# Weight sums of two feed-forward tiles moved from engines to adding DMAs, block sums of the normed tokens moved to VectorE, two results written in place

## The chip, the cores and the metric

The kernel runs on one core of one Trainium2 chip. The metric is the device time of one execution in microseconds, given as the median over runs; less is better. Arithmetic is fp32; for the matmuls every operand is split into a high and a low part of type fp32r.

## The reference, cut to what matters

An encoder trunk of two layers works on 512 + 256 tokens of width 1024. Each layer has a mixer (attention and an mLSTM, side by side), a residual with layer norm, a gated feed-forward of width 2816 with a convolution over three neighbouring tokens, and a second residual with layer norm. The change is all in the feed-forward and in the step into it:

```python
x = _layer_norm(ALPHA * x + mix, ln1_g, ln1_b)
gu = x @ w_gu
gate, up = gu[..., :D_FF], gu[..., D_FF:]
conv = conv_b + sum(gp[:, j:j + S] * conv_w[j] for j in range(CONV_WIDTH))   # gp: gate, padded by a token at each end
hmid = gelu(conv) * up
x = _layer_norm(ALPHA * x + hmid @ w_down, ln2_g, ln2_b)
```

## The kernel before, in words

The 768 tokens are 6 token tiles of 128, the feed-forward's width is 22 tiles of 128. Each operand of a matmul stands twice, as a high part and as the remainder, and each product takes three passes (high by high, high by low, low by high).

The gate and up products of one feed-forward tile are one two-by-two block product in Strassen's form: with the token halves (tiles 0 to 2 and 3 to 5) and the two halves of the contraction there are seven products `p1` to `p7` of 12 matmuls each (`product`, line 967) instead of eight. Their operands are sums. On the weights' side four are needed for each feed-forward tile: t1 = u0 + g0, t2 = u1 + t1, t3 = u1 + u0, t4 = g1 + t2. On the tokens' side there are four sums for each token tile of the second half (`combine`, lines 905 to 908), made once in a layer. `ff_tile` puts the seven results together: the copy `m1` of `p1` (line 979, ScalarE), `u2`, `u4`, `u3` (lines 988, 989, 992) and from these the halves of `g` and `up` (lines 983, 993, 996, 999), all on VectorE, then the convolution (lines 1000 to 1003), gelu (1004), the product (1005) and its split (1009, 1010). After every three tiles `down` (line 1027) adds their part of the second product to the accumulator.

Class `Weights` brings the weights. Pieces of 128 x 512 are loaded in a fixed order on SyncE's queue into a ring of six raw slots (line 143). Each block is then converted: ScalarE makes the high part (line 186), VectorE the remainder (line 187), into one of 12 slots. Sums are made in two ways. For feed-forward tiles 1 and 2 (`ENG`) engines make them from raw pieces (`_value`, line 164): t1 and t3 on GpSimd, t2 and t4 on VectorE, into one buffer `E` or over a raw piece. For all other tiles a DMA on SyncE's queue copies one summand into a slot `T` (line 152), and a DMA on GpSimd's queue adds the other (line 153). There are four slots `T` (`NSUM`); the load of a sum waits until the sum four places earlier has been converted. They exist from the start of the output projection of the mixer to the end of the feed-forward.

Step into the feed-forward: the second half of the output projection (`wo`, line 923) goes over the token tiles in the order 0, 1, 3, 2, 4, 5. For each, VectorE adds the residual (926), takes statistics (865, 870), GpSimd makes the inverse deviation (871, 872), and VectorE applies the norm (876, 882). Then `combine` makes the four sums of tiles 3, 4 and 5, on VectorE for the tiles in `VT` and else on GpSimd. Two token tiles later the blocks are transposed on TensorE (386), and split on ScalarE (388) and VectorE (389). The first two products of feed-forward tiles 0 and 1 (`FF_EARLY`) are started ahead of the rest.

The order on each engine is set when the program is built: an instruction's priority is its place in the code, shifted by `prio` (conversions are put back by 100, the first products forward by 50). An engine then works in that order. PSUM banks are taken in turn by tag (`FTAGS`: three `d`, two `s`, one `L`), so a product waits until the results of an earlier one have been read. In `ff_tile` every buffer exists once; the copy `m1` of tile 1 waits for the last reader of `m1` of tile 0.

Of the kernel before, what the change touches and what calls it, by code (L numbers as in the profile page):

```python
# [13 lines left out]
F32 = mybir.dt.float32  # L14
F32R = mybir.dt.float32r
AF = mybir.ActivationFunctionType
ALU = mybir.AluOpType
# [16 lines left out]
HALF = T // 2  # L34
# [49 lines left out]
WO_K = (4,5,0,1,6,7,2,3)  # L84
WO_ORDER0 = (0, 1, 2, 3, 4, 5)
NSG = 3
NSUM = 4
ENG = (1, 2)
AT1 = 11
AT2 = 8  # L90
AT3 = 12
FF_EARLY = 2
WO_ORDER = (0,1,3,2,4,5)
LAG1 = 2
VT = (5,)


class Weights:

# [15 lines left out]

    def block(self, src, n, dst=None):
        self.blocks.append((src, n, dst))  # L120
        for x in (src["a"], src["b"]) if isinstance(src, dict) and src["engine"] else (src,):
            if not isinstance(x, dict):
                self.uses[x] += 1

    def sum(self, layer, a, b, engine=None, over=None):

        s = {"a": a, "b": b, "engine": engine, "layer": layer, "read": False, "over": over}
        if engine is None:
            self.sums.append(s)
        return s  # L130

    def unit(self, ap, n=1024):
# [5 lines left out]
    def _load(self):  # L138

        while self.n_dma < len(self.dram) and (self.n_dma < NRAW or self.uses[self.n_dma - NRAW] == 0):  # L140
# [4 lines left out]
            self.n_dma += 1  # L145
        while self.diff_pool is not None and self.n_sum < len(self.sums) and (self.n_sum < NSUM or self.sums[self.n_sum - NSUM]["read"]):
            s = self.sums[self.n_sum]
            if s["layer"] != self.layer:
                break
            s["tile"] = t = self.diff_pool.tile([128, 512], F32, tag="T", name=f"T{self.n_sum}", bufs=NSUM)  # L150
            self.n_sum += 1
# [1 line left out]
            self.nc.gpsimd.dma_start(t, s["b"]["tile"] if isinstance(s["b"], dict) else s["b"], accum_op=ALU.add)  # L153

    def _value(self, src, n):
        if isinstance(src, dict):
            if "tile" not in src:

                v = [x["tile"] if isinstance(x, dict) else self.raw[x] for x in (src["a"], src["b"])]
                if isinstance(src["b"], dict) or src["over"]:  # L160
                    src["tile"] = v[1]
                else:
                    src["tile"] = self.diff_pool.tile([128, 512], F32, tag="E", name=f"E{self.n_conv}", bufs=1)
                src["engine"].tensor_tensor(out=src["tile"], in0=v[0], in1=v[1], op=ALU.add)
                for x in (src["a"], src["b"]):
                    if not isinstance(x, dict) and x != src["over"]:
                        self.uses[x] -= 1
            return src["tile"]
        return self.raw[src]

    def _conv(self, i):
        src, n, dst = self.blocks[i]
        self._load()
        v = self._value(src, n)
        if callable(dst):
            dst(v)
            self.uses[src] -= 1
            return
        if dst is None:
            h = self.hl_pool.tile([128, WCOL], F32R, tag="wh", name=f"wh{i}")[:, :n]  # L180
            l = self.hl_pool.tile([128, WCOL], F32R, tag="wl", name=f"wl{i}")[:, :n]
            self.hl[i] = (h, l)
        else:
            h, l = dst
            v = v.rearrange("p (k t) -> p k t", k=4)
        self.nc.scalar.activation(h, v, AF.Identity)  # L186
        self.nc.vector.tensor_tensor(out=l, in0=v, in1=h.bitcast(F32), op=ALU.subtract)  # L187
        if isinstance(src, dict):
            src["read"] = True
            if src["over"]:  # L190
                self.uses[src["over"]] -= 1
        else:
            self.uses[src] -= 1
        self._load()

    def pump(self):

        live = sum(1 for j in range(self.n_done, self.n_conv) if self.blocks[j][2] is None)
        while self.n_conv < len(self.blocks):
            if isinstance(self.blocks[self.n_conv][0], dict):  # L200
                self._load()
                if self.diff_pool is None or ("tile" not in self.blocks[self.n_conv][0] and not self.blocks[self.n_conv][0]["engine"]):
                    break
            if self.blocks[self.n_conv][2] is None:
                if live >= NSLOT:
                    break
                live += 1
            with self.prio(self.urgency):
                self._conv(self.n_conv)
            self.n_conv += 1  # L210
# [16 lines left out]
def trunk(ctx, nc, tc, d, o, depth=DEPTH):  # L227
    V, S, G, PE = nc.vector, nc.scalar, nc.gpsimd, nc.tensor
# [18 lines left out]
    def P(tag, name):  # L247
        return pp.tile([128, 512], F32, tag=tag, name=name, bufs=banks[tag])
# [10 lines left out]
    W = Weights(nc, wr, wh, prio)  # L259
# [27 lines left out]
    for l in range(depth):  # L287
        if l:
            for u in range(4):
                W.unit(d["w_c1"][l, u], 1056)  # L290
        for u in range(4):
            W.unit(d["w_av"][l, u])
        for h in range(4):
            W.unit(d["w_aq"][l, h])
            W.unit(d["w_ak"][l, h])
            if h == 0 or h == (1 if L1 else 2):
                for u in range(4):
                    W.unit(d["w_lv" if h == 0 else "w_lo"][l, u])
        for hf in range(2):
            for u in range(4):  # L300
                W.unit(d["w_out"][l, hf, u])
        early = {}
        for i in range(FF_EARLY):
            early[i] = [W.piece(d["w_g"][l, i, :, p * 512:(p + 1) * 512], 512) for p in range(2)]
            for src in early[i]:
                W.block(src, 512)
        for kind, i in ffn_seq:
            if kind == "f":


                def at(w, p):
                    return d[w][l, i, :, p * 512:(p + 1) * 512]

                g0, g1 = early[i] if i in early else [W.piece(at("w_g", p), 512) for p in range(2)]
                if i in ENG:
                    u0, u1 = [W.piece(at("w_u", p), 512) for p in range(2)]
                    t1 = W.sum(l, u0, g0, G)
                    t2 = W.sum(l, u1, t1, V)
                    t3 = W.sum(l, u1, u0, G, over=u0)
                    t4 = W.sum(l, g1, t2, V)  # L320
                else:
                    u1 = W.piece(at("w_u", 1), 512)
                    t1 = W.sum(l, at("w_u", 0), at("w_g", 0))
                    t2 = W.sum(l, at("w_u", 1), t1)
                    t3 = W.sum(l, at("w_u", 1), at("w_u", 0))
                    t4 = W.sum(l, at("w_g", 1), t2)
                for src in (t1, t2, t3, t4, u1) if i in early else (g0, g1, t1, t2, t3, t4, u1):
                    W.block(src, 512)
            else:
                f0, f1 = FF_GROUPS[i]  # L330
                for hf in range(2):
                    for f in range(f0, f1):
                        W.block(W.piece(d["w_down"][l, f, :, hf * 512:(hf + 1) * 512], 512), 512)
# [58 lines left out]
    for l in range(depth):  # L392
# [503 lines left out]
        def combine(t):  # L896
# [5 lines left out]
            x0, x1 = acc[:, t - 3, 0:512], acc[:, t - 3, 512:1024]  # L902
            E = V if t in VT else G
            s1, s2, s3, s4 = (sp.tile([128, 512], F32, tag=f"S{i}", name=f"S{i}_{t}") for i in (1, 2, 3, 4))
# [11 lines left out]
        for hf in range(2):  # L916
            order = (WO_ORDER0, WO_ORDER)[hf]
            units = [W.take() for _ in range(8)]
            for j, t in enumerate(order):
                p = P("d", f"wo{hf}{t}")  # L920
# [28 lines left out]
        ft = FT.enter_context(tc.tile_pool(name=f"ft{l}", bufs=1, reuse_waits="tile"))  # L949
# [8 lines left out]
        def bank(name):  # L958
            n_bank[0] += 1
            return P(tags[(n_bank[0] - 1) % 6], name)[:, 0:HALF]  # L960

        def product(ps, x):

            blk = W.take()
            for k in range(4):
                for i, (a, b) in enumerate(PASSES):
                    PE.matmul(ps, blk[1 + a][:, k * 128:(k + 1) * 128], x[:, k, b, :], start=k + i == 0, stop=k == 3 and i == 2)  # L967
            W.done(blk)

        def ff_tile(f):  # L970
            w0, w1, w2, cb = (convw[:, l, f, i:i + 1] for i in range(4))
            g = ft.tile([128, T], F32, tag="g", name=f"g{f}")
            up = ft.tile([128, T], F32, tag="up", name=f"up{f}")
            c = ft.tile([128, T], F32, tag="c", name=f"c{f}")
            m1, u2, u3, u4 = (ft.tile([128, HALF], F32, tag=t, name=f"{t}_{f}") for t in ("m1", "u2", "u3", "u4"))
            lo_, hi_ = slice(0, HALF), slice(HALF, T)
            p1 = bank(f"p1_{f}")
            product(p1, A11)
            S.copy(m1, p1)
# [26 lines left out]
            s = f % RING  # L1006
# [5 lines left out]
        def down(gi):  # L1012
# [5 lines left out]
            for hf, t in ([(hf, t) for t in range(NT) for hf in range(2)] if last else [(hf, t) for hf in range(2) for t in range(NT)]):  # L1018
# [18 lines left out]
                if last and hf:  # L1037
# [8 lines left out]
                    else:  # L1046
                        dst = o["out_1_dram"][rows] if t < SB // 128 else o["out_0_dram"][t * 128 - SB:t * 128 - SB + 128]
                        for i in range(parts):
                            c = slice(i * 1024 // parts, (i + 1) * 1024 // parts)
                            (nc.sync, nc.scalar)[i % 2].dma_start(dst[:, c], acc[:, t, c])  # L1050

        started = {i: ff_tile(i) for i in range(FF_EARLY)}
        for i in range(FF_EARLY):
            with prio(PR_E):
                next(started[i])
        W.urgency = PR_CONV2
        for kind, i in ffn_seq[:-1]:
            if kind == "f":
                for _ in started.pop(i) if i in started else ff_tile(i):
                    pass  # L1060
            else:
                down(i)
# [81 lines left out]
```

## Time and profile before

| | us |
|---|---|
| median of 3 runs | 1808.9 |
| lowest, highest | 1808.42, 1810.11 |
| profiled execution, its own time | 1809.26 |
| span of the profile | 1807.5 |
| TensorE busy in the span | 1770.1 |
| VectorE busy | 1270.8 |
| ScalarE busy | 774.5 |
| GpSimd busy | 273.7 |

The span goes from the first to the last instruction; the execution's own time has 1.8 us around it. Busy times are shares of the whole run, which has stages with different limits. The first step into the feed-forward lies at about 363 to 412 us, the second at 1260 to 1309 us.

### The profile page before, as it was taken

To read this page: it belongs to the slowest core of one execution; us is meant where nothing else is said; L and a number is where in the kernel's file an instruction comes from. 1 tells how busy PE (TensorE), PEld (TensorE's weight loads), DVE (VectorE), ACT (ScalarE), POOL (GpSimd) and SP (SyncE) were. 2 spreads that over 40 slices of the span, in tenths; PEclk is the share of its full clock that TensorE was granted. 3 is DMA by queue.
4 is the path that set the end of the run, shared out by engine and by line. 5 is a ranking of instruction groups with operands and counts; after the bars stand their busy time and mean duration, and the time that the engine had idled before them with its cause. 6 is when DMAs were issued, how large, how long until landed. Compare 5 with 4: busy or idle time off the path is not lost. (4 is left out here: it accounts for less than half of the span.)

```text
span 1807.5 us, 26787 instructions
## 1 busy us (share of the span) xinstructions
PE 1770.1 (98%) x9692; PEld 1578.8 (87%) x9692; DVE 1270.8 (70%) x2512; ACT 774.5 (43%) x1636; POOL 273.7 (15%) x346
## 2 busy tenths in 40 slices
PE   8999999999999999999999999999999999999998
PEld 8877887889899899899898778878899899898996
DVE  5546887489677577576955468875996676676778
ACT  4445667135334244244323556671453343342340
POOL 2001011241111111110020011102411111111102
PEclk9999999999999999999999999999999999999999
DMA  5312221625666566565232213134356575565631
GB/s 190 101 53 71 73 63 56 189 53 147 143 154 169 121 164 162 124 164 135 88 106 71 62 55 94 48 101 139 76 150 144 129 185 135 134 175 125 155 105 70
DMA packets 129556, 211.55 MB, mean 117 GB/s; under 512 B 12272, under 2 KB 37488, under 8 KB 129424
## 3 DMA queue, kind: packets, MB, share of 16 engines
q1 hardware_dynamic: 105664, 167.51, 29.4%
q0 software_dynamic: 23040, 41.95, 13.9%
q8 instruction: 76, 1.25, 0.3%
q14 instruction: 56, 0.46, 0.1%
q10 hardware_dynamic: 720, 0.37, 0.1%
HBM read 182.43 MB, written 6.39 MB: 104 GB/s over the span
## 5 line engine op out<-in xcount | busy, mean ns | idle before, releaser
L967 PE MATMUL p<-actA,wh 128*128 128x384 f32 x1408 | 362.9, 338 | 0.0
L186 ACT ACTIVATE wh<-raw 128x512 fp32r<-128x512 f32 (+1 forms) x352 | 218.9, 630 | 303.6 <-PE p L967 130.6
L187 DVE TENSOR_TENSOR wl<-raw,wh 128x512 fp32r<-128x512 f32 (+1 forms) x352 | 244.5, 704 | 78.2 <-ACT wh L186 77.6
L967 PE MATMUL p<-actB,wh 128*128 128x384 f32 x1056 | 272.4, 338 | 4.0 <-DVE up L993 3.6
L967 PEld LDWEIGHTS p<-actA,wh 128*128 128x128 f32 x1408 | 254.8, 188 | 1.9 <-DVE acc L926 0.5
L967 PE MATMUL p<-actA,wl 128*128 128x384 f32 x704 | 237.2, 337 | 0.0
L186 ACT ACTIVATE wh<-T 128x512 fp32r<-128x512 f32 x160 | 100.2, 630 | 275.6 <-PE dn L1027 126.0
L1027 PE MATMUL dn<-wh,actB 128*128 128x512 f32 x576 | 207.8, 394 | 0.0
L967 PEld LDWEIGHTS p<-actB,wh 128*128 128x128 f32 x1056 | 192.1, 189 | 5.2 <-DVE up L993 4.3
L1027 PE MATMUL dn<-wh,ring 128*128 128x512 f32 x480 | 178.1, 395 | 0.0
L967 PE MATMUL p<-actB,wl 128*128 128x384 f32 x528 | 177.9, 338 | 0.0
L1034 DVE TENSOR_TENSOR acc<-acc,dn 128x512 f32<-128x512 f32 x144 | 98.3, 685 | 90.6 <-PE dn L1027 90.5
L187 DVE TENSOR_TENSOR wl<-T,wh 128x512 fp32r<-128x512 f32 x160 | 111.8, 705 | 38.2 <-ACT wh L186 38.0
L967 PEld LDWEIGHTS p<-actA,wl 128*128 128x128 f32 x704 | 132.2, 188 | 0.0
L1027 PEld LDWEIGHTS dn<-wh,actB 128*128 128x128 f32 x576 | 108.1, 188 | 25.5 <-ACT actB L1009 0.8
L923 PE MATMUL wo<-wh,actB 128*128 128x512 f32 x384 | 122.9, 397 | 0.0
L153 POOL DMA_DIRECT2D T<-T x80 | 70.0, 875 | 298.4 <-issue 65.0
L1027 PE MATMUL dn<-wl,actB 128*128 128x512 f32 x288 | 113.3, 393 | 0.0
L1027 PEld LDWEIGHTS dn<-wh,ring 128*128 128x128 f32 x480 | 90.2, 188 | 20.7
L153 POOL DMA_DIRECT2D T<-in_w_g_dram x40 | 35.5, 888 | 467.9 <-DMA T<-in_w_u_dram 256.9
L967 PEld LDWEIGHTS p<-actB,wl 128*128 128x128 f32 x528 | 99.7, 189 | 0.0
L1027 PE MATMUL dn<-wl,ring 128*128 128x512 f32 x240 | 94.9, 395 | 0.0
(275 smaller groups left out, 3442.1 us busy)
## 6 DMA issues: line engine op xcount, KB each, us to landing
T<-in_w_u_dram SPq DMA_DIRECT2D x120, 256.0 KB, 2.9
raw<-in_w_g_dram SPq DMA_DIRECT2D x88, 256.0 KB, 3.4
raw<-in_w_down_dram SPq DMA_DIRECT2D x88, 256.0 KB, 3.3
T<-T POOLq DMA_DIRECT2D x80, 256.0 KB, 4.4
raw<-in_w_u_dram SPq DMA_DIRECT2D x48, 256.0 KB, 3.2
T<-in_w_g_dram SPq DMA_DIRECT2D x40, 256.0 KB, 3.9
T<-in_w_g_dram POOLq DMA_DIRECT2D x40, 256.0 KB, 4.6
T<-in_w_u_dram POOLq DMA_DIRECT2D x40, 256.0 KB, 5.8
```

Of the source, the lines that this page charges most:

```text
L153: self.nc.gpsimd.dma_start(t, s["b"]["tile"] if isinstance(s["b"], dict) else s["b"], accum_op=ALU.add)
L186: self.nc.scalar.activation(h, v, AF.Identity)
L187: self.nc.vector.tensor_tensor(out=l, in0=v, in1=h.bitcast(F32), op=ALU.subtract)
L923: PE.matmul(p, actB[:, k, a, t * 128:(t + 1) * 128], units[k][1 + b], start=n + i == 0, stop=n == 7 and i == 2)
L967: PE.matmul(ps, blk[1 + a][:, k * 128:(k + 1) * 128], x[:, k, b, :], start=k + i == 0, stop=k == 3 and i == 2)
L1027: PE.matmul(p, x, (wh_, wl_)[b], start=k + i == 0, stop=k == nf - 1 and i == 2)
L1034: V.tensor_tensor(out=z, in0=z, in1=p, op=ALU.add)
```

## The change: what it does

All weight sums are made by the two DMAs; `ENG` and the engines' way are gone. There are six slots `T` instead of four, and no buffer `E`. The block sums of token tiles 3 and 4 are made by VectorE, as those of tile 5 were. `u2` is written over `m1`, and `u3` into the second half of `g`, which saves two buffers of 128 x 384.

```diff
-NSUM = 4
-ENG = (1, 2)
+NSUM = 6
-VT = (5,)
+VT = (3, 4, 5)
     def block(self, src, n, dst=None):
         self.blocks.append((src, n, dst))
-        for x in (src["a"], src["b"]) if isinstance(src, dict) and src["engine"] else (src,):
-            if not isinstance(x, dict):
-                self.uses[x] += 1
-
-    def sum(self, layer, a, b, engine=None, over=None):
+        if not isinstance(src, dict):
+            self.uses[src] += 1
+
+    def sum(self, layer, a, b):
 
-        s = {"a": a, "b": b, "engine": engine, "layer": layer, "read": False, "over": over}
-        if engine is None:
-            self.sums.append(s)
+        s = {"a": a, "b": b, "layer": layer, "read": False}
+        self.sums.append(s)
         return s
...
     def _value(self, src, n):
-        if isinstance(src, dict):
-            if "tile" not in src:
-
-                v = [x["tile"] if isinstance(x, dict) else self.raw[x] for x in (src["a"], src["b"])]
-                if isinstance(src["b"], dict) or src["over"]:
-                    src["tile"] = v[1]
-                else:
-                    src["tile"] = self.diff_pool.tile([128, 512], F32, tag="E", name=f"E{self.n_conv}", bufs=1)
-                src["engine"].tensor_tensor(out=src["tile"], in0=v[0], in1=v[1], op=ALU.add)
...
+        return src["tile"] if isinstance(src, dict) else self.raw[src]
...
                 g0, g1 = early[i] if i in early else [W.piece(at("w_g", p), 512) for p in range(2)]
-                if i in ENG:
-                    u0, u1 = [W.piece(at("w_u", p), 512) for p in range(2)]
-                    t1 = W.sum(l, u0, g0, G)
-                    t2 = W.sum(l, u1, t1, V)
-                    t3 = W.sum(l, u1, u0, G, over=u0)
-                    t4 = W.sum(l, g1, t2, V)
-                else:
-                    u1 = W.piece(at("w_u", 1), 512)
-                    t1 = W.sum(l, at("w_u", 0), at("w_g", 0))
-                    t2 = W.sum(l, at("w_u", 1), t1)
-                    t3 = W.sum(l, at("w_u", 1), at("w_u", 0))
-                    t4 = W.sum(l, at("w_g", 1), t2)
+                u1 = W.piece(at("w_u", 1), 512)
+                t1 = W.sum(l, at("w_u", 0), at("w_g", 0))
+                t2 = W.sum(l, at("w_u", 1), t1)
+                t3 = W.sum(l, at("w_u", 1), at("w_u", 0))
+                t4 = W.sum(l, at("w_g", 1), t2)
...
-            m1, u2, u3, u4 = (ft.tile([128, HALF], F32, tag=t, name=f"{t}_{f}") for t in ("m1", "u2", "u3", "u4"))
+            m1, u4 = (ft.tile([128, HALF], F32, tag=t, name=f"{t}_{f}") for t in ("m1", "u4"))
             lo_, hi_ = slice(0, HALF), slice(HALF, T)
+            u2, u3 = m1, g[:, hi_]
```

## Rows read from the trace of the kernel before

**Rows 1.** The page's head and its line of the engines.
```profile
span 1807.5 us, 26787 instructions
PE 1770.1 (98%) x9692; PEld 1578.8 (87%) x9692; DVE 1270.8 (70%) x2512; ACT 774.5 (43%) x1636; POOL 273.7 (15%) x346
```

**Rows 2.** Busy time by stretch: stretch, its length, PE, PEld, DVE, ACT, POOL, clock, DMA.
```profile
455.00:890.00 435.00, 435.00 (x2258) 402.60 (x2257) 306.78 (x516) 159.12 (x259) 61.62 (x74) 1.00 0.58 143
...
1259.70:1309.00 49.30, 46.70 (x266) 40.78 (x264) 44.66 (x65) 20.30 (x36) 22.48 (x22) 1.00 0.29 70
363.00:412.30 49.30, 46.68 (x267) 40.79 (x265) 44.70 (x65) 20.28 (x36) 22.41 (x22) 1.00 0.28 70
```

**Rows 3.** Waits of PE, whole run: us in total, times, longest.
```profile
PE p L967 <- DVE up L993: 3.6, 2, 1.8
...
PE p L967 <- ACT actB L388: 0.3, 2, 0.2
```

**Rows 4.** Timeline of PE at its gaps: start, duration, instructions, idle time before.
```profile
412.29 0.62 PE L967 MATMUL p<-actB,wh 128*128 128x384 f32 x2 [1.81 <-DVE up L993]
...
1275.40 0.66 PE L386 MATMUL y1T<-ident,S 128*128 128x128 f32 x4 [0.56 <-DVE actA L389]
...
1309.02 0.62 PE L967 MATMUL p<-actB,wh 128*128 128x384 f32 x2 [1.84 <-DVE up L993]
```

**Rows 5.** Busy time by stretch, after the stall of layer 1 (columns as above).
```profile
1309.30:1313.30 4.00, 4.00 (x15) 4.00 (x15) 3.97 (x9) 1.52 (x2) 0.00 (x0) 0.57 0.01 4
1313.30:1317.30 4.00, 4.00 (x24) 4.00 (x24) 2.06 (x4) 3.60 (x6) 0.00 (x0) 1.00 0.00 0
```

**Rows 6.** Timeline of DVE: conversions, the middle ones just ahead of line 993.
```profile
1280.12 2.50 DVE L187 TENSOR_TENSOR wl<-T,wh 128x512 fp32r<-128x512 f32 x2
...
1304.44 4.06 DVE L187 TENSOR_TENSOR wl<-raw,wh 128x512 fp32r<-128x512 f32 x3
...
1342.32 1.28 DVE L187 TENSOR_TENSOR wl<-raw,wh 128x512 fp32r<-128x512 f32 x2
```

**Rows 7.** Timeline of POOL: block sums and weight sums.
```profile
1268.91 2.29 POOL L908 TENSOR_TENSOR S<-S,acc 128x512 f32<-128x512 f32 x1
...
1280.34 1.73 POOL L907 TENSOR_TENSOR S<-acc 128x512 f32<-128x512 f32 x1
1282.03 1.73 POOL L906 TENSOR_TENSOR S<-S,acc 128x512 f32<-128x512 f32 x1
...
1304.61 1.66 POOL L164 TENSOR_TENSOR E<-raw,raw 128x512 f32<-128x512 f32 x1 [4.35 <-DVE wl L187]
1306.35 1.60 POOL L164 TENSOR_TENSOR raw<-raw,raw 128x512 f32<-128x512 f32 x1
```

**Rows 8.** Timeline of DVE: two of its idle times.
```profile
1266.17 0.69 DVE L926 SCALAR_TENSOR_TENSOR acc<-acc,wo 128x512 f32<-128x512 f32 x1 [1.20 <-PE wo L923]
...
1272.14 1.28 DVE L882 SCALAR_TENSOR_TENSOR acc<-acc,rsa,lnb 128x1024 f32<-128x1024 f32 x1 [2.10 <-POOL rsa L872]
```

**Rows 9.** GpSimd's additions (ns shortest/median/longest), and its accumulating DMAs (busy, mean ns).
```profile
L164 POOL TENSOR_TENSOR E<-raw,raw x4: 1283/1484/1677, 349.4 to 1304.6; 128x512 f32<-128x512 f32 x4
...
L153 POOL DMA_DIRECT2D T<-T x80 | 70.0, 875 | 298.4 <-issue 65.0
```

**Rows 10.** SP's issues on its timeline; DMA issues of 1280 to 1305, us to landing.
```profile
1281.00 13.09 SPq L152 DMA_DIRECT2D T<-in_w_u_dram  x3
...
T<-in_w_u_dram SPq DMA_DIRECT2D x3, 256.0 KB, 2.5
T<-T POOLq DMA_DIRECT2D x2, 256.0 KB, 3.9
T<-in_w_u_dram POOLq DMA_DIRECT2D x1, 256.0 KB, 5.8
```

**Rows 11.** Timeline of ACT and DVE: the copy of `m1` of tile 1, and line 992.
```profile
1301.27 0.48 ACT L979 COPY m<-p 128x384 f32<-128x384 f32 x1 [0.31 <-DVE u L988]
...
1303.37 0.55 DVE L992 TENSOR_TENSOR u<-p,u 128x384 f32<-128x384 f32 x1
```

More of the change, by code (lines that the diff above doesn't have):

```diff
@@ L155, in _value @@
     def _value(self, src, n):
-        if isinstance(src, dict):
-            if "tile" not in src:
-                v = [x["tile"] if isinstance(x, dict) else self.raw[x] for x in (src["a"], src["b"])]
-                if isinstance(src["b"], dict) or src["over"]:
-                    src["tile"] = v[1]
-                else:
-                    src["tile"] = self.diff_pool.tile([128, 512], F32, tag="E", name=f"E{self.n_conv}", bufs=1)
-                src["engine"].tensor_tensor(out=src["tile"], in0=v[0], in1=v[1], op=ALU.add)
[L165 to L169, printed above, removed]
+        return src["tile"] if isinstance(src, dict) else self.raw[src]
     def _conv(self, i):
@@ L189, in _conv @@
             src["read"] = True
-            if src["over"]:
-                self.uses[src["over"]] -= 1
         else:
@@ L201, in pump @@
                 self._load()
-                if self.diff_pool is None or ("tile" not in self.blocks[self.n_conv][0] and not self.blocks[self.n_conv][0]["engine"]):
+                if self.diff_pool is None or "tile" not in self.blocks[self.n_conv][0]:
                     break
```

## The prediction

> **What bounds the kernel now.** I began with the engine line of the page: TensorE is busy 1770.1 of 1807.5 us [rows 1]. An edit that touches neither the matmuls nor their number can only win back TensorE's idle time, some 37 us over the whole run, and only where it stands near the edit. The table of stretches says where that is: the long feed-forward of a layer has 435.00 busy us in 435.00, so six slots or better sums can win nothing there, while the 49.3 us from the third normed token tile to the first feed-forward tile hold 46.7 busy us in either layer [rows 2]. There VectorE is busy 44.7 us, so both engines are nearly full.
>
> The waits of TensorE name a stall that the edit can reach: twice 1.8 us, released by `up` in line 993 [rows 3]. TensorE's timeline places it, 1.81 us ahead of 412.29 and 1.84 us ahead of 1309.02, and shows a second kind: 0.56 us ahead of 1275.40, on a transposed split of line 389 [rows 4] (layer 0 has the like). After the stall of layer 1 the granted clock is at the half level, 1.2 of 2.4 GHz, for a while: 4 us held 15 matmuls where the next 4 us, at the full level, held 24, one every 0.17 us [rows 5]. Layer 0 had the same stall and kept its clock.
>
> Why line 993 is late is read on VectorE and GpSimd side by side. Line 993 frees the PSUM bank of `p5` of tile 0, which a product of tile 1 wants. Ahead of it in VectorE's order stand three conversions (line 187) that took 4.06 us together, where two such took 1.28 us elsewhere [rows 6]. In just that time GpSimd ran two sums of line 164, at 1304.61 and 1306.35 [rows 7]. The pair of conversions at 1280.12, which took 2.50 us [rows 6], ran beside GpSimd's subtractions of lines 907 and 906 [rows 7]. So a GpSimd addition out of SBUF costs a conversion that meets it about 0.6 to 1.1 us. The 0.56 us has another cause: VectorE sat idle 2.10 us until line 872 [rows 8], because GpSimd had the four block sums of token tile 3 ahead of it, the last from 1268.91 to 1271.20 [rows 7].
>
> **Part by part, for one layer.**
> *Sums of tiles 1 and 2 by DMA.* Four GpSimd additions of 1.28 to 1.68 us go [rows 9], and four of VectorE, of the shape of a conversion: some 0.60 us from one start to the next, since two undisturbed conversions take 1.28 us with a little overlap [rows 6]. Two of these stand ahead of line 993: 1.2 us. With the GpSimd additions the three conversions ahead of line 993 fall from 4.06 to about 1.9 us: 2.2 us. Added are eight copies on SP's queue and eight accumulating DMAs on GpSimd's; a copy lands after 2.5 us, an accumulation after 3.9 to 5.8 us [rows 10]. Each holds GpSimd for 0.9 us [rows 9], hidden, since it has nothing else in the feed-forward. On SP two raw loads go; the raw loads behind the copies are wanted tens of us later.
>
> *Six slots.* The first two sums of tile 1 are loaded beside tile 0's, long before use. Its third and fourth wait until tile 0's first two sums are converted (SP's loads of line 152 already take 13.09 us for three, waiting for such slots [rows 10]). I price the latest case. TensorE comes to tile 1 half a microsecond before the stall, at 1306.7 [rows 4]; `p5` of tile 0 begins 60 matmuls of 0.17 us and a few transposes earlier, at 1296 or so, and both move 0.6 us ahead with the first gap. By 1295.4 the first sum must be converted; then 2.5 us copy, 0.9 us issue, 5.8 us accumulation [rows 9, 10] and 1.3 us for both halves of the conversion give 1305.9, against 1306.1. Even this case fits, so I take 0; the upper bound is 2 us, if both DMAs take their longest and the queue on GpSimd is met.
>
> *Block sums on VectorE.* Eight more operations (tiles 3 and 4) at 0.60 us are 4.8 us. Returned are 1.2 us of the pair at 1280.12, 2.2 us and 1.2 us from above: VectorE's 44.7 us become 44.7 + 4.8 - 4.6 = 44.9, to be fitted into 49.3 us less what I win (2.4): 96%. What hides the added work is idle time of its own: 1.20 us at 1266.17 and 2.10 us at 1272.14 [rows 8], of which the second goes because GpSimd's `rs` is no longer behind the sums. If that cover were gone, it would cost up to 3.6 us (4.8 less the two additions). For token tile 4 the sums end earlier than on GpSimd, at 0.60 us instead of 1.73 [rows 7]. What is late next are the conversions of tile 0's own sums, which now fall behind the sums of tile 4.
>
> *Two results in place.* `m1` stays in use until line 992 instead of line 988, so the copy of `m1` for tile 1 (ACT, 1301.27, released by line 988) moves behind line 992 (1303.37 to 1303.92), to about 1304.0 to 1304.5 [rows 11]. That copy frees the bank that `p3` of tile 0 wants, 12 matmuls of 0.17 us ahead of 1306.7: at 1304.7. Queued behind it on ACT are tile 1's conversions. Nearest row, no stall; upper bound 1.9 us, if three conversions stand ahead of line 992. A gain is excluded, since it only adds a wait. I take 0. In all later tiles the copy comes many us after line 992. `g` costs nothing: its old readers are waited for already.
>
> **The sum.** Stalls on line 993: 2 x 1.8 = 3.6 us. Stalls on line 389: 2 x 0.56 = 1.1 us. Half clock in layer 1: 9 matmuls fewer in 4 us, 9 x 0.17 = 1.5 us. Total 6.2 us. The profiled execution took 1809.26 us, 1.8 us more than its span and 0.4 us above the median of 1808.9; 1809.26 - 6.2 = 1803.1. Own range of this case: 1800.5 (counted from start to start the two long stalls are 2.0 us instead of 1.8, and the waits on `actB`, 0.3 us in all [rows 3], and other gaps as short, some 2 us together, could go too) to 1805.2 (a third of the gain comes back as waits).
>
> **Rivals.**
> *A new wait takes the stall's place, no change.* The bank of `p3` through the later copy of `m1`, at its bound of 1.9 us in each layer: 2 x 1.9 back, the clock dip with it (1.5): 6.2 - 5.3 leaves 0.9, so 1808.4. For it: in the trace lines 989 and 992 already stand behind two conversions and an addition, and the backlog of conversions comes first in VectorE's order. Against: TensorE's order can put another product there.
>
> *The sums of tile 1 come late.* At the bound of 2 us in each layer 4.0 us come back: 1807.1, no change. For it: slots are freed by conversions, which the change defers, and GpSimd's DMAs could have to wait for gaps in VectorE's work, of which few are left. Against: even the latest case just fits, and between 1280 and 1305, with VectorE almost full, such DMAs landed after 3.9 to 5.8 us [rows 10]. So I give it 6 in 100. One rule of the Trainium skill speaks for this rival ("SBUF — State Buffer", the box on DVE blocking a DMA): while VectorE runs in a two-port mode, GpSimd cannot write the descriptors of a DMA it issues; by it the time would be the 1807.1 above, and the landings just named do not show it.
>
> *VectorE becomes the bound, slower.* Place: the chain of token tile 5 (lines 926, 876, 882, 905 to 908, 389) and the conversions before `p5` of tile 0. Price: if neither the slowed conversions nor the idle time come back, 3.6 us in each layer stand on the path, the stalls remain, 1809.3 + 7.2 = 1816.5; with half of it 1813. It decides as soon as VectorE's work in the 49.3 us passes TensorE's 46.7. For it: 44.9 us is close, with waits inside. Against: the slow conversions coincide with GpSimd's additions to the microsecond.
>
> *The change does not do what it says:* the order of the engines comes out anew and another conversion delays line 993: 1809, no change.
>
> **How the numbers follow.** Main case 0.66, its own range 1800.5 to 1805.2; bank of `p3` 0.10; late sums 0.06; order 0.07; VectorE 0.11. A measurement here can tell about 0.2%, 3.6 us: faster means below 1805.3, slower above 1812.5. Faster: the main case and a little of the others that stop halfway, 0.68. Same: 0.21. Slower: 0.11. The range reaches to the cases of no change, 1800.5 to 1809.3, and leaves out the slower ones and the far low end.
>
> **What would show it.** Right: no line 164 any more, no operation of GpSimd between lines 905 and 908, the conversions ahead of line 993 at 0.68 us each; no wait of TensorE on line 993 and no half clock near 1310; VectorE about 45 us busy in the stretch; TensorE's idle time down by 4 to 5 us. Wrong: a wait of `p` on the copy of line 979 or on what it waits for, of line 186 on a DMA into `T` near the first two tiles, or new gaps of TensorE ahead of `p5`. A loss inside the 435 us that were full would upset the reading altogether.

## The result, and the profile after

The changed kernel takes 1829.76 us (median of 4 runs, 1827.98 to 1831.88) against 1809.34 before: ratio 1.0109, 95% interval 1.0097 to 1.0121. It is 20 us slower where 6 us less was forecast. Medians and ratios here and below are of runs in the fast state; two of the seven runs of the version e11 below (2481 and 4214 us) were slow and are left out. The profiled execution took 1831.88 us. The head of its page and its line of the engines answer to [rows 1]:

```profile
span 1829.8 us, 26947 instructions
...
PE 1776.3 (97%) x9692; PEld 1585.4 (87%) x9692; DVE 1270.9 (69%) x2520; ACT 778.3 (43%) x1636; POOL 251.1 (14%) x338
```

VectorE's work is the same to 0.1 us and GpSimd's is 22.6 us less, as the change meant. TensorE's busy time grew by 6.2 us with the same instructions, and its idle time by 16.1 us. The table of stretches (columns as in [rows 2]) says where:

```profile
468.00:903.00 435.00, 435.00 (x2257) 402.57 (x2257) 306.96 (x516) 160.83 (x259) 58.65 (x70) 1.00 0.56 140
1272.80:1322.10 49.30, 46.25 (x265) 40.86 (x264) 43.27 (x68) 19.60 (x35) 6.10 (x12) 1.00 0.22 55
366.30:415.60 49.30, 45.51 (x261) 40.05 (x259) 42.95 (x67) 19.63 (x35) 5.69 (x12) 1.00 0.23 54
...
400.00:412.50 12.50, 11.42 (x69) 10.76 (x68) 8.40 (x15) 3.10 (x6) 2.68 (x3) 1.00 0.67 170
412.50:425.00 12.50, 9.04 (x42) 8.40 (x41) 5.65 (x10) 4.19 (x8) 3.55 (x4) 0.86 0.94 221
...
425.00:437.50 12.50, 8.82 (x42) 8.50 (x41) 11.56 (x22) 8.00 (x13) 3.53 (x4) 0.86 0.91 218
```

The long feed-forward is full as before, and the 49.3 us of [rows 2] lost only 0.5 and 1.2 busy us. The loss stands just behind them, in the first three feed-forward tiles: 25 us with 17.9 busy us, a clock of 0.86, and the DMA engines 91 to 94% busy. The kernel before, in the two corresponding stretches:

```profile
410.00:422.50 12.50, 10.69 (x61) 10.37 (x60) 11.28 (x20) 5.33 (x8) 1.21 (x1) 1.00 0.10 31
422.50:435.00 12.50, 12.50 (x74) 12.50 (x73) 12.40 (x24) 9.44 (x17) 0.00 (x0) 1.00 0.43 139
```

Counted by the start of the first product of each layer: layer 0 begins 2.3 us late (388.14 against 385.81), layer 1 13.1 us late (1295.60 against 1282.54), and the span ends 22.3 us late. So either layer loses about 10 us. The first 2.3 us stand ahead of the change (between 100 and 300 us TensorE is already busy 2.8 us less than before); over all the profiled runs below that start lies between 384.2 and 390.6.

TensorE's waits, as in [rows 3] (line 941 was 967, `up` of line 993 is now line 968, `g` of line 958 was line 983; line 967 was 992 and makes `u3`, which now lies in `g`):

```profile
PE p L941 <- DVE g L958: 7.9, 2, 4.2
...
PE p L941 <- DVE g L967: 6.8, 2, 3.4
...
PE p L941 <- ACT actA L362: 1.9, 4, 0.7
...
PE p L941 <- DVE m L963: 0.7, 1, 0.7
```

The wait on `up` is gone, as predicted; two that are twice as long took its place in either layer. TensorE's timeline in layer 0, as in [rows 4]:

```profile
411.99 0.59 PE L941 MATMUL p<-actB,wh 128*128 128x384 f32 x2 [0.74 <-DVE m L963]
...
417.22 1.01 PE L941 MATMUL p<-actA,wh 128*128 128x384 f32 x2 [3.40 <-DVE g L967]
...
429.63 0.61 PE L941 MATMUL p<-actB,wh 128*128 128x384 f32 x2 [3.68 <-DVE g L958]
```

After either long gap the clock is at the half level. The stretch behind the first one, to set against [rows 5]:

```profile
417.20:420.40 3.20, 3.18 (x10) 3.18 (x11) 1.04 (x2) 0.00 (x0) 0.98 (x2) 0.50 0.83 218
```

Ten matmuls took 3.2 us instead of 10 x 0.175: 1.45 us lost. It happens after all four long gaps, so at least 5.8 us (the last, behind 1336.36, lasts longer: 18 matmuls in 5.64 us, 2.5 us lost), where the kernel before lost 1.5 us once.

Why lines 967 and 958 are late is read on ScalarE and VectorE. ScalarE's timeline (line 169 is the first half of a conversion, line 954 the copy of `m1`):

```profile
410.02 0.63 ACT L169 ACTIVATE wh<-T 128x512 fp32r<-128x512 f32 x1 [6.13 <-DMA T<-in_w_u_dram]
413.08 0.63 ACT L169 ACTIVATE wh<-T 128x512 fp32r<-128x512 f32 x1 [2.43 <-DMA T<-T]
...
422.73 0.63 ACT L169 ACTIVATE wh<-T 128x512 fp32r<-128x512 f32 x1 [6.94 <-DMA T<-T]
423.26 0.46 ACT L954 COPY m<-p 128x384 f32<-128x384 f32 x1
...
427.76 0.63 ACT L169 ACTIVATE wh<-T 128x512 fp32r<-128x512 f32 x1 [1.69 <-DMA T<-T]
```

VectorE's timeline (line 170 is the second half):

```profile
399.40 0.68 DVE L170 TENSOR_TENSOR wl<-T,wh 128x512 fp32r<-128x512 f32 x1
...
410.68 0.69 DVE L170 TENSOR_TENSOR wl<-T,wh 128x512 fp32r<-128x512 f32 x1 [3.20 <-ACT wh L169]
411.29 0.55 DVE L963 TENSOR_TENSOR m<-m,p 128x384 f32<-128x384 f32 x1
413.74 0.69 DVE L170 TENSOR_TENSOR wl<-T,wh 128x512 fp32r<-128x512 f32 x1 [1.90 <-ACT wh L169]
...
416.62 0.55 DVE L967 TENSOR_TENSOR g<-p,m 128x384 f32<-128x384 f32 x1
...
423.39 0.69 DVE L170 TENSOR_TENSOR wl<-T,wh 128x512 fp32r<-128x512 f32 x1 [5.16 <-ACT wh L169]
424.00 0.55 DVE L971 TENSOR_TENSOR g<-p,g 128x384 f32<-128x384 f32 x1
...
428.42 0.69 DVE L170 TENSOR_TENSOR wl<-T,wh 128x512 fp32r<-128x512 f32 x1
429.03 0.55 DVE L958 TENSOR_TENSOR g<-p,m 128x384 f32<-128x384 f32 x1
```

Both engines sit idle until a DMA has landed in `T`, and what stands behind the conversion in their order are results of other tiles that TensorE waits for: line 967 of tile 0 behind the fourth sum of tile 1, and line 958 of tile 1 behind tile 2's sums, twice over. The copy of `m1` that it reads stands on ScalarE behind the second sum; with that copy done at 423.72, line 958 still stands on VectorE behind the conversions of the second, third and fourth sum and behind tile 0's convolution (lines 977 and 978), whose start on ScalarE waits behind the third. The table of DMA issues for 400 to 437.5 gives the landings (KB, median us), as in [rows 10]:

```profile
T<-in_w_u_dram SPq DMA_DIRECT2D x10, 256.0 KB, 4.0
T<-T POOLq DMA_DIRECT2D x5, 256.0 KB, 6.1
...
T<-in_w_u_dram POOLq DMA_DIRECT2D x3, 256.0 KB, 6.7
T<-in_w_g_dram POOLq DMA_DIRECT2D x3, 256.0 KB, 7.0
```

In the median an addition now lands after 6.1 to 7.0 us where [rows 10] had 3.9 and 5.8, a copy after 4.0 instead of 2.5.

### The profile page after: what moved, and what is told of

Its sections match the earlier page's. It is cut to its first block, busy times and chain, and to the rows that moved or that the text cites. A ratio compares the mean times of both kernels' runs of the same rounds, so it can differ in the third digit from the quotient of the medians.

```text
span 1829.8 us, 26947 instructions
## 1 busy us (share of the span) xinstructions
PE 1776.3 (97%) x9692; PEld 1585.4 (87%) x9692; DVE 1270.9 (69%) x2520; ACT 778.3 (43%) x1636; POOL 251.1 (14%) x338
## 5 line engine op out<-in xcount | busy, mean ns | idle before, releaser
L170 DVE TENSOR_TENSOR wl<-raw,wh 128x512 fp32r<-128x512 f32 (+1 forms) x348 | 237.3, 692 | 87.8 <-ACT wh L169 87.1
L169 ACT ACTIVATE wh<-T 128x512 fp32r<-128x512 f32 x176 | 111.3, 632 | 299.8 <-PE p L941 133.0
L170 DVE TENSOR_TENSOR wl<-T,wh 128x512 fp32r<-128x512 f32 x176 | 120.0, 689 | 39.9 <-ACT wh L169 39.7
L149 POOL DMA_DIRECT2D T<-T x88 | 77.8, 884 | 271.7 <-DMA T<-in_w_g_dram 86.6
L149 POOL DMA_DIRECT2D T<-in_w_u_dram x44 | 40.8, 928 | 409.5 <-DMA T<-in_w_u_dram 242.0
```

## The experiments

Each time is the median, each ratio that to the kernel before, run on the same chip (median there 1809.4 to 1811.0). Differences of two kernels are read from their ratios or medians; a run's own profile is named where rows come from it.

**Block sums, places and slots one by one.** Four runs ask whether the block sums on VectorE put everything late, or the late weight sums do it by themselves.

e1, from the changed kernel:
```diff
-VT = (3, 4, 5)
+VT = (5,)
```


> The changed kernel, with the block sums of token tiles 3 and 4 back on GpSimd (VT = (5,)); adding DMAs, six slots and results in place stay. Theory A (the third and fourth sum of feed-forward tile 1 get their slot only when tile 0's sums are converted, and the conversions that wait for them stand ahead of tile 0's results on ScalarE and VectorE; what makes them so late is the block sums that now hold VectorE): the first conversions of tile 0's sums come some 15 us earlier, as before, the two long waits of TensorE in each layer (3.4 and 3.7 to 4.2 us, with the half clock after them) go, and the time is within 4 us of the kernel before, 1805 to 1813. Theory B (six slots are too few whatever VectorE does, since they hold only two sums of tile 1 from the start): the waits stay, 1824 to 1832. Theory C (the result in place, m1 held longer, makes the waits): they stay as well, but on line 954 rather than on a DMA.

Measured: 1825.72 us, 1.0089 (1.0074 to 1.0104). Tile 0's first sum is converted early again (1292.96, ahead of layer 1's first product at 1295.38), and the gap before line 967 goes. The other becomes longer:

```profile
PE p L941 <- DVE g L958: 10.7, 2, 5.5
```

The time is in the range of theory B and not of A, though one of the two waits went as A has it: the block sums on VectorE cost some 4 us of the 20, no more. Tile 2's sums, which take the slots of tile 0's third and fourth (converted at 1306.77 and 1309.16), stay late: the first of their additions is issued at 1310.72 and lands at 1316.47.

e2, from the kernel before: `VT = (3, 4, 5)` alone.

> The kernel before with the block sums of token tiles 3 and 4 on VectorE (VT = (3, 4, 5)) and nothing else of the change. Theory A: the conversions of tile 0's sums are late here too, but tile 1's sums come from the engines, so nothing of tile 1 waits for a DMA: the 0.56 us waits on transposed blocks shrink, the 1.8 us wait on the bank of p5 stays within 1 us; 1805 to 1811. Rival (VectorE is the bound once it has the block sums): 1813 or more.

Measured: 1814.85 us, 1.0024 (1.0014 to 1.0033), slower. Line 993 is waited for no more, but:

```profile
PE p L967 <- DVE g L983: 5.3, 2, 2.7
PE p L967 <- ACT actA L388: 1.9, 4, 0.7
```

Tile 0's first sum is converted at 1297.52 instead of 1280.12 [rows 6], the four copies into slots that wait for this leave SP's queue at 1298.27 to 1303.41, and their additions follow on GpSimd's queue. There GpSimd's own additions for tile 2 stand behind them and begin only at 1313.66: just ahead is the addition into tile 3's fourth sum, issued at 1313.09, which needs the second sum, and that one was issued at 1307.44 and took 4.9 us to land. The results behind the conversions of tile 2's sums wait in turn. The time lies in the rival's range, but not for the rival's reason: VectorE sits idle 3.11 us up to 1315.98, waiting for ScalarE's half of a conversion of such a sum. So the deferral that the prediction called "late next" costs on its own.

e3, from the kernel before: the two results in place (the last hunk of the diff) alone.

> The kernel before with u2 written over m1 and u3 into the second half of g, and nothing else. Theories A and B: no change, within 2 us of 1809.3, with the wait on the bank of p5 as before. Theory C (m1 in use until line 992 delays the copy of tile 1 and with it the bank of p3): 1.9 us more in each layer, 1813.

Measured: 1809.91 us, 0.9999 (0.9988 to 1.0009). No effect, as predicted.

e4, from the kernel before:
```diff
-ENG = (1, 2)
+ENG = ()
```


> The kernel before with ENG empty: all sums by adding DMAs in four slots, block sums and results as before. Theory A (block sums on VectorE are what makes the conversions late): all four sums of tile 1 now wait for tile 0's conversions, which come early as before, at about 1281 of the second layer, so that the sums land by 1300; some wait is left, 1808 to 1816. Theory B (slots that hold too little): worse than the changed kernel, which has two sums of tile 1 loaded ahead: 1830 or more.

Measured: 1828.61 us, 1.0103 (1.0086 to 1.012). The time lies between the two ranges, close to theory B's. All sums by DMA give almost the whole loss with GpSimd's block sums and four slots:

```profile
PE p L967 <- DVE up L993: 12.9, 4, 4.2
```

**Which sums.** e5, from the changed kernel, leaves the eight sums of tiles 1 and 2 out: one summand is loaded in each one's place, so the output differs.
```diff
-                u1 = W.piece(at("w_u", 1), 512)
...
+                if i in (1, 2):
+                    t1, t2, t3, t4, u1 = [W.piece(at(w, p), 512) for w, p in (("w_u", 0), ("w_u", 1), ("w_u", 1), ("w_g", 1), ("w_u", 1))]
```


> The changed kernel, in which the four weight sums of feed-forward tiles 1 and 2 are left out: one summand each is loaded into a raw slot in their place; block sums on VectorE, six slots for the other tiles and results in place stay. Theory A (the sums of tiles 1 and 2 land late because their slots come free late, and their conversions stand in the order of ScalarE and VectorE ahead of results that TensorE waits for): those conversions wait for nothing but raw loads, so the two long waits of each layer and the half clock after them go; what is left is the change without its sums, 1800 to 1808. Rival D (block sums on VectorE and results in place hold the path themselves, whatever the sums do): 1814 or more, as with the block sums alone.

Measured: 1812.03 us, 1.001 (1.0001 to 1.0019). Without these sums 18 of the 20 us are gone, though the time lies above theory A's range. A gap of 2.0 us is left in either layer: ScalarE waits up to 409.18 for a raw load of `w_g`, issued at 403.37. Ahead of it on SP's queue stand copies of tile 3's and tile 4's summands that waited for slots until 401.25, and the first conversion that frees a raw slot there ended at 403.30; which of the two held it is not shown, but both wait for conversions that came late.

e6 and e7 sum tile 2 alone by DMA, from the kernel before; e7 with six slots and the results in place besides, e8 is e7 with the block sums on VectorE.
```diff
-NSUM = 4
-ENG = (1, 2)
+NSUM = 6
+ENG = (1,)
...
-VT = (5,)
+VT = (3, 4, 5)
```
(e6 has the line of `ENG` only, e7 the first two, e8 all three.)

> The kernel before with ENG = (1,): only tile 2's sums go over to adding DMAs, four slots, block sums and results as before. Theory A: they get the slots of tile 0's sums, whose conversions free two slots at about 1281 and two at 1294 to 1297 of the second layer; they land by 1304 and are wanted after 1310, so nothing waits for them, and the two GpSimd additions beside the three conversions ahead of line 993 are gone: the 1.8 us wait goes, 1803 to 1807. Rival E (adding DMAs are too slow in this stretch wherever their slots come from): a wait of ScalarE on a DMA into T before 1330, 1812 or more.

> As e6, with six slots and with u2 and u3 in place: two of tile 2's sums are loaded with tile 0's. Theory A: as e6 or up to 1 us better, 1802 to 1807; rival E: 1810 or more.

> As e7, with the block sums of token tiles 3 and 4 on VectorE as well, so that of the change only tile 1's sums by DMA are missing. Theory A: the conversions of tile 0's sums come some 15 us later, so that the third and fourth sum of tile 2 get their slots at about 1297 and land at 1306 to 1312, before they are wanted; the time is that of e7 within 2 us. Rival D: 4 us or more above e7.

Measured: e6 1813.55 us, 1.0022 (1.0013 to 1.003); e7 1805.64 us, 0.998 (0.9971 to 0.9989); e8 1805.67 us, 0.9976 (0.9966 to 0.9985). e7 and e8 are the only versions faster than both kernels. With four slots e6 misses its range and comes out in rival E's: it wins the stall at 1309 and loses more behind tile 3's sums, for which ScalarE waits up to 1325.03, 1327.24 and 1330.83 (a gap of TensorE of 2.49 us at 1340.98). In e7 six slots undo that (the results in place alone change nothing, e3), so rival E does not hold with six slots. The block sums on VectorE neither cost nor win anything there (e8 against e7). In e8 the long waits are gone, and one kind is left:

```profile
PE p L967 <- ACT actA L388: 1.9, 4, 0.7
```

So what the prediction hoped to win was there to be won, most of it (the waits on line 388 came in place of those on line 389), as long as tile 1's sums were not in the queue.

e12, from e8:
```diff
-ENG = (1,)
+ENG = (2,)
```


> Six slots, block sums on VectorE, results in place; tile 1's sums by DMA, tile 2's on the engines as before. If tile 1's sums alone are late: the first stall of each layer (3.4 us, and 1.5 us at the lower clock) stays and the second (3.7 to 4.3) goes, 1815 to 1820. If it is the number of sums in the queue together: both go, 1804 to 1807. If tile 1's sums make both: 1826 to 1830.

Measured: 1815.85 us, 1.0035 (1.0022 to 1.0049). The first of the two stalls stays and the second is gone (line 993 of this kernel makes `u3`; it is line 992 of the kernel before and 967 of the changed one):

```profile
PE p L967 <- DVE g L993: 6.6, 2, 3.5
```

So tile 1's sums make the first stall, some 10 us of the 24 that lie between e8 and the changed kernel. Tile 2's make the second, the rest, but only behind tile 1's: without those in the queue (e8) they cost nothing.

**Order or slots.** e9, from the changed kernel, defers the conversions in the written order, behind tile 0's last results; e11 does the same to e8.
```diff
-PR_CONV1 = -100
-PR_CONV2 = -100
+PR_CONV1 = -200
+PR_CONV2 = -200
```


> The changed kernel with one thing altered: the conversions of the sums of tiles 1 and 2 are placed later in the written order, so that on VectorE the conversions of tile 1's and tile 2's last sums stand behind tile 0's results, and on ScalarE tile 1's first copy of a product stands ahead of the conversion of tile 1's third sum. Theory (in-order engines: late conversions stand ahead of tile 0's results, which TensorE waits for): the two stalls of each layer shrink, and the time falls by 6 to 12 us against the changed kernel, to 1818 to 1824. Rival (TensorE truly lacks these sums, wherever their conversion stands): the stalls move to the products that want the sums, and the time stays at 1828 to 1832.

> As the run with six slots, block sums on VectorE, and tile 2's sums alone by DMA (1805.7), with the conversions placed later in the written order. If a late conversion still stands ahead of a result there, 1802 to 1805; if nothing is late any more, 1805 to 1807, no difference.

Measured: e9 1823.41 us, 1.008 (1.0066 to 1.0094), 5 to 6 us better. The wait on line 967 is gone, but the other grew:

```profile
PE p L941 <- DVE g L958: 13.0, 2, 7.2
...
PE p L941 <- DVE up L968: 1.4, 1, 1.4
```

This order is worth 5 to 6 us, at the low end of what was expected. It does not show what the best order would give: tile 0's convolution still stands on ScalarE behind tile 2's second sum (converted at 417.07, after 4.38 us of waiting), and line 958 on VectorE behind that. e11 came out at 1815.11 us, 1.003 (1.0017 to 1.0043), some 10 us worse than e8, which neither expectation had. In its profile TensorE waits for line 994 (`up`, 2.7 us) and for the sums of the second matrix (3.2 us); that later conversions free slots later, and so make the tiles behind late, is argued and not shown.

e10, from the changed kernel: `NSUM = 7` (three of tile 1's sums begun ahead).

> The changed kernel with seven slots in place of six, so that three of tile 1's sums are begun ahead. Theory (a slot is had only when tile 0's first conversions free one, and the sums that wait for it land late): one sum fewer is late in each layer, and the time falls by 3 to 6 us against the changed kernel, to 1824 to 1827. Rival (the rate of the transfers is the bound, not the slots): no change, 1828 to 1832.

Measured: 1828.63 us, 1.0108 (1.0093 to 1.0124): nothing. A reason that fits is in the stretches of its profile, where the DMA engines are busy all the time:

```profile
409.80:422.30 12.50, 9.48 (x46) 8.60 (x44) 4.09 (x8) 3.14 (x6) 4.48 (x5) 0.88 1.01 247
422.30:434.80 12.50, 8.84 (x41) 8.59 (x41) 10.65 (x20) 7.81 (x13) 3.56 (x4) 0.84 0.98 237
```

**Rate or chain.** e13, from the changed kernel, adds only 32 of the 128 partitions (three quarters of each addition are left out, so the output differs); number, order and slots stay.
```diff
-            self.nc.gpsimd.dma_start(t, ..., accum_op=ALU.add)
+            self.nc.gpsimd.dma_start(t[:32], (...)[:32], accum_op=ALU.add)
```


> The changed kernel, whose adding transfers carry only 32 of the 128 partitions: the other three quarters of the additions into the sums are left out. Number and order of the transfers, slots and engine orders stay. In the changed kernel the DMA engines are busy 91 to 94% of the 25 us in which the late sums are loaded (the kernel before: 10 to 43%). Theory (the transfers' rate makes the sums late; the late start for want of slots only pushes them into that stretch): the additions land in 2 to 4 us instead of 6 to 8, the stalls mostly go, 1808 to 1816. Rival (the chain of slot, copy and addition makes them late, whatever the size): 1825 to 1831.

Measured: 1814.62 us, 1.0026 (1.0015 to 1.0037), 15 us better with the same chain of waits. TensorE's waits, to set against those of the changed kernel:

```profile
PE p L941 <- DVE g L967: 4.0, 2, 2.0
...
PE p L941 <- DVE g L958: 1.0, 2, 0.6
```

Its DMA issues in the corresponding 25 us, from 398 to 423:

```profile
T<-T POOLq DMA_DIRECT2D x5, 64.0 KB, 4.1
...
T<-in_w_g_dram POOLq DMA_DIRECT2D x3, 64.0 KB, 4.1
```

Additions that carry a quarter land after 4.1 us instead of 6 to 7, and of the two long gaps in either layer 2.0 us are left of the first (line 967) and 0.6 us or less of the second (line 958). So most of the loss is the load of the additions on the DMA engines, put into too short a time; bytes and packets fall together here, so the run does not tell which of them counts. The chain of slot, copy and addition keeps the first gap open: tile 1's fourth sum lands at 408.60, 4.14 us after its addition was issued, with ScalarE waiting for it.

e14, from e10: `VT = (5,)`, so that the first slots come free earlier and there are seven.

> The changed kernel with seven slots and with the block sums of token tiles 3 and 4 back on GpSimd, so that the first slots come free some 10 us earlier and one sum more is begun ahead. Each alone gained 0 (seven slots) and 4 us (block sums). If the rate of the transfers over too short a stretch is what costs: together they spread the sums over a longer time, 1813 to 1820. If tile 2's sums still get their slots only from tile 1's conversions: 1822 to 1827, as with block sums alone.

Measured: 1821.03 us, 1.0063 (1.0045 to 1.008). The seventh slot, worth nothing in e10, is worth some 5 us beside e1 once the transfers that wait for a slot begin earlier (the first at 1289.12 in layer 1, at 1303.04 in e10). The time lies between the two ranges, a little short of what a pure rate would give. All sums by DMA stayed slower than the kernel before in every form that was run.

## Why the prediction was wrong

*What bounds the kernel* held: the long feed-forward stayed full, the gain in reach was the stalls on lines 993 and 389, and e8 won 4 us of the 6.2 forecast in the median (5.4 in its span) when the first of these went.

*Sums of tiles 1 and 2 by DMA*: what it removes was right. Line 993 is waited for no more, and the 12 conversions out of `T` in the late stretch take 685 ns each. What it adds was read from the wrong rows. The landings of 3.9 and 5.8 us came from 1280 to 1305 [rows 10], where the DMA engines were half busy:

```profile
1280.00:1305.00 25.00, 24.78 (x153) 22.70 (x152) 23.88 (x38) 11.48 (x21) 10.40 (x11) 1.00 0.49 111
```

The change itself puts six copies and six additions of these two tiles, 3 MB (the other two sums are begun ahead), into some 25 us, with tile 3's first and raw loads beside them, where the engines are then 91 to 94% busy. And raw loads behind the copies were not always wanted "tens of us later": in e5 ScalarE waits 7.80 us for one, up to 409.18.

*Six slots* is the step that failed ("even this case fits, so I take 0; the upper bound is 2 us"). It asked of one sum, the third of tile 1, whether it would come in time for the product that wants it. It priced that one about right. Its deadline for the start was kept: tile 0's first sum was to be converted by 12.9 us after the first product (1295.4 against 1282.54), and VectorE took it up 11.3 us after (399.40 against 388.14). Copy, issue and addition then took 9.9 us (400.16 to 410.02) where the step has 9.2, and that sum cost 0.7 us in layer 0, nothing in layer 1. Three things were not in the step. The next sums queue behind it at the same two queues and the same DMA engines: tile 1's fourth, then tile 2's, whose first copy begins 3.6 us after the first of tile 1's (403.75 against 400.16). What a late sum holds up is not the product that wants it but whatever stands behind its conversion on ScalarE and VectorE; there it is the results of an earlier tile, and TensorE runs out of PSUM banks. And each of the four long gaps brought the clock down behind it. Against the bound of 2 us stand per layer, from the rows above, 0.7 + 3.4 + 3.7 idle us and 2 x 1.45 us of clock in layer 0: 10.7.

*Block sums on VectorE*: its time was covered, as worked out. "What is late next are the conversions of tile 0's own sums" named the right victim and priced it at nothing; e2 measures 0.24% for it, since the slots hang on those conversions, and on the slots tile 3's sums and what stands behind them on GpSimd's queue. The gap of 0.56 us on line 389 went, but waits on line 362 (1.9 us in all) came for it, so the 1.1 us of this term were not won.

*Two results in place*: 0, as predicted (e3).

The rival of the late sums was right in kind, and at 6 in 100 and 2 us a layer some five times too small. Its condition, slots freed late because the change defers conversions, makes only some 4 us of the 20 (e1): with the first conversions early again, and in e4 with the block sums on GpSimd throughout, the sums came late all the same. The rule quoted for it, the Trainium skill's "SBUF — State Buffer" (the box on DVE blocking a DMA), does not account for it: additions issued at 415.51, 416.16 and 418.28 took 7.1, 8.3 and 7.4 us to land, in the 12.5 us where VectorE is busy only 5.65, and the first two issues held GpSimd for 0.87 and 1.13 us, about as in [rows 9]; no run shows whether VectorE was ever in such a mode. Another page of the Trainium skill, "DMA: Bandwidth & Descriptors" (the anatomy of one DMA on GpSimd's path), gives a fit of 2.0 us plus the bytes at 436 GB/s, an estimate of 2.6 us for 256 KB; no adding transfer of this size seen here was as fast (the fastest took 3.2 us), and in the full stretch the medians are 6.1 to 7.0 us. The rivals of VectorE's bound, of `p3`'s bank and of the order anew do not show: in the 49.3 us VectorE is busy 43 us, less than before.

What e13 still lacks against e8 is 9 us in the ratios, 10.7 in the two profiles' spans. Of the latter 5.2 are idle time of TensorE in the first 100 us from each layer's first product (the gaps of 2.0 and 0.6 us above all), 2.1 a longer busy time, with the clock at 0.98 in those 100 us of layer 1, and 3.4 idle time in other stages. Open is what the best order of the conversions would give with all sums by DMA, and whether bytes, packets or GpSimd's queue make the additions slow.

## What to carry to other kernels

When additions move from an engine to adding DMAs, add up the bytes against the time between the moment the buffers come free and the moment of use, with the landing times of a full DMA stretch and not of a half-empty one. Then ask of every conversion that waits for a transfer what else stands behind it on its engine: in a fixed order a late load stops the results of tiles that have all they need. Moving the second tile's sums alone, with two slots more, won 0.2% here; moving the first's alone lost 0.35%, and moving both lost 1.1%.

## What was not expected of the hardware

An adding transfer on GpSimd's queue took more of the DMA engines' time than a plain one of the same size on SP's. The table of queues for 400 to 437.5 of the changed kernel (packets, MB, share of the time of 16 engines):

```profile
q1 hardware_dynamic: 2747, 5.01, 44.1%
q0 software_dynamic: 1416, 2.59, 39.9%
```

GpSimd's queue, which holds the additions, took 15.4% for each MB, SP's, with copies and raw loads, 8.8%: 1.75 times as much. In the kernel before, from 1280 to 1305, it is 1.6 times (24.1% for 1.05 MB against 24.4% for 1.70). No run separates the addition from the queue.

How long TensorE stood idle does not alone decide whether its clock falls. In the kernel before, a gap of 1.84 us brought the half level and one of 1.81 us did not ([rows 4, 5], and the clock of 1.00 in the stretch from 410.00 shown with the result); in e12 a gap of 3.52 us in layer 0 brought it, one of 3.06 us in layer 1 did not, though it is longer than the 1.84. Stretches behind the last two, columns as in [rows 5]:

```profile
415.88:419.08 3.20, 3.20 (x10) 3.20 (x11) 2.68 (x5) 1.54 (x3) 1.09 (x2) 0.53 0.89 197
1315.58:1318.78 3.20, 3.20 (x18) 3.20 (x19) 3.17 (x7) 1.54 (x3) 1.69 (x2) 1.00 1.01 262
```

So a stall of this size costs its own length, or 1.5 us and more besides, and a forecast should carry both.
